# Two chains for the sums of squares, weight sums in small tiles, and other parts, in a two-layer hybrid decoder

## The chip, the cores and the metric

The kernel runs on one core of a Trainium2 chip. TensorE (PE, with its weight loads as PEld), VectorE (DVE), ScalarE (ACT) and GpSimd (POOL) each work through a queue of their own in order; transfers are issued from SyncE's queue (SP) and from GpSimd's. The metric is the device time of one execution in microseconds, the median of the runs.

## The reference

512 tokens of width 1024 pass through two layers, everything in float32:

```python
x = x + 0.5 * swiglu(rmsnorm(x, norm_ffn1[l]), w_ffn1_in[l], w_ffn1_out[l])
h = rmsnorm(x, norm_mix[l])
x = x + mixing_sublayer(h, w_in[l], ...)     # retention (4 heads) and forgetting attention (8 heads), gated
x = x + 0.5 * swiglu(rmsnorm(x, norm_ffn2[l]), w_ffn2_in[l], w_ffn2_out[l])
...
def rmsnorm(x, g): return x * rsqrt(mean(x * x) + EPS) * g
def swiglu(h, w_in, w_out):
    a, b = split(h @ w_in)                   # 2 x 2816 columns
    return (silu(a) * b) @ w_out
```

The output is rmsnorm of the last x.

## The kernel before

x is kept transposed, as eight tiles `x0` to `x7` of 128 channels by 512 tokens. Each float32 product is done as three matmuls of rounded halves: `split` makes the high half on ScalarE (a CAST, `wH`, `uH`, `xh`, `mh`) and the rest on VectorE (`wL`, `uL`, `ml`).

**FFN.** The 22 blocks of 128 hidden columns are taken in groups of four (some of two), and groups are put together into parts (`FF_PARTS`): a part's input products are followed by its output products (`po`), four times two blocks of x (`mi`). The input products of a group (`ffn_group`) are done as a 2 x 2 Strassen-like scheme: seven products of sums of weight quarters (`A12`, `A11`, `A22`, and the sums `S1`, `S3`) with seven forms of x (`b21`, `n11`, `m1` to `m4`, `b22`), into the banks Y, X and W. `prep_forms(n, l, k)` makes the forms of x tiles k and k+4, when these are done. `S1` and `S3` are made by a load of one quarter from SP and a transfer from GpSimd that adds another one (`summed`, L386); VectorE makes further sums with `more` (L425). A group's first weights, A12, are split into tiles of a ring: `wtile(w, ring[0])` takes every fourth pair of halves from the `y` tiles of the mixer and the forms, the others from the `wH` and `wL` tiles.

**Raw weights** lie in tiles that depend on `places`, and in two large `wst` tiles. With `aside`, in a group that follows the mixer and in the first of all, S1 lies in `wide` tiles.

**Statistics.** For the rmsnorm, `square` writes the square of each x tile (from three `r` tiles) on ScalarE and adds it to the first square, `sqa`, by a transfer from GpSimd. `rstd` sums `sqa` over its partitions with four matmuls `xs` (L315), then takes the root on GpSimd. In the mixer, R is the row of roots, sent to DRAM and read back for all partitions.

**Mixer** (`mix`): retention's values first (`rv_units`: 48 matmuls `pv` on the first half of the input blocks, then 48 on the second), then its heads, then the eight heads of forgetting attention, the gates and the outputs (`pyr`, `pyf`), and the product with `w_out` (`pw`), after which the forms of ffn2 are made.

The order on each engine is made from this code by a scheduler that may move instructions ahead of those that wait.

Of the kernel before, what the change touches and what calls it, by code (L numbers as in the profile page):

```python
# [6 lines left out]
F32 = mybir.dt.float32  # L7
FR = mybir.dt.float32r
AF = mybir.ActivationFunctionType
ALU = mybir.AluOpType  # L10
# [11 lines left out]
NFF = DFF // P  # L22
FF_PARTS = (((0, 4), (4, 4)), ((8, 4), (12, 4)), ((16, 2), (18, 4)))
FF_FIRST = (((2, 4),), ((6, 4), (10, 4)), ((14, 4), (18, 4)))
RH = 4
FH = 8
FD = 64
# [14 lines left out]
def trunk(  # L42
# [103 lines left out]

    xs = [st("x", f"x{m}") for m in range(KD)]
    xH, xL = [None] * KD, [None] * KD
    sqa = [None]


    def split(src, hi, lo, lo_eng=None):
# [25 lines left out]
        return w  # L178

    ALL = slice(None)  # L180

    def pair(nm, parts, nk=KD):

# [20 lines left out]
    def proj_tok(o, b, w, k0, nk, last_k, mvH, mvL):  # L204

        h, lo = w
        bs = slice(b * P, (b + 1) * P)
        for k in range(nk):
            kk = k0 + k
            PE.matmul(o, mvH[kk][:, bs], h[:, k], start=kk == 0, stop=False)  # L210
            PE.matmul(o, mvH[kk][:, bs], lo[:, k], start=False, stop=False)
            PE.matmul(o, mvL[kk][:, bs], h[:, k], start=False, stop=kk == last_k)  # L212


    def square(src, first):
        sq = st("r", "sq")
        S.activation(sq, src, AF.Square)
        if first:
            sqa[0] = sq
        else:  # L220
            G.dma_start(sqa[0], sq, accum_op=ALU.add)

    def prep(n, l, m):
        g = gain(n, l, m)
# [7 lines left out]
        square(src, m == 0)  # L232

# [15 lines left out]
    def prep_forms(n, l, k, first=False):  # L249

        if k == 0:
            tags[0] = iter(FIRST_TAGS if first else FORM_TAGS)
            forms.clear()
        x1, x2 = xs[k], xs[k + 4]
        H2 = T // 2
        b2 = st2(next(tags[0]), f"b2_{k}")
        scaled(b2[:, 0:T], b2[:, T:2 * T], x2, gain(n, l, k + 4))
        if k % 2 == 0:
            forms["n1", k // 2] = st2(next(tags[0]), f"n1_{k}")
        n1 = forms["n1", k // 2][:, (k % 2) * T:(k % 2 + 1) * T]  # L260
# [13 lines left out]
        V.scalar_tensor_tensor(  # L274
            out=m4, in0=x2[:, 0:H2], scalar=gain(n, l, k + 4), in1=m2,
            op0=ALU.mult, op1=ALU.subtract,
        )
        mh, ml = st2(next(tags[0]), f"mh{k}"), st2(next(tags[0]), f"ml{k}")
        split(mt, mh, ml)
        for q in range(2):  # L280
            def at(t, c):
                return t[:, c + q * P:c + (q + 1) * P]
            forms["b21", k, q] = at(b2, 0), at(b2, T)
            forms["b22", k, q] = at(b2, H2), at(b2, T + H2)
            forms["n11", k, q] = at(n1, 0), at(n1, H2)
            for i in range(4):
                forms[f"m{i + 1}", k, q] = at(mh, i * H2), at(ml, i * H2)
        if not first:
            square(x1, k == 0)
            square(x2, False)  # L290

    def to_dram(cols, n, nm):

# [61 lines left out]
    def ffn_group(w, f, n, todo, rtok, aside):  # L355
# [3 lines left out]
        nh = 4 // nk  # L359
        ca, cb = f * P, DFF + f * P  # L360

        def piece(r, c, s):
            return rows(w, r + s * nk * P, r + (s + 1) * nk * P, c, c + cw)

        def v3(t):
            return t.rearrange("p (k c) -> p k c", k=nk)

        def place(nm, tag=None):
            tag = tag or places[nm]
            nm = f"{nm}_{f}"  # L370
            if tag == "wst":
                t = wp.tile([P, 2048], F32, tag="wst", bufs=2, name=f"wst_{nm}")
                return [t[:, s * 1024:(s + 1) * 1024] for s in range(nh)]
            if tag == "wide":
                return [wide(f"{nm}_{s}")[:, 0:1024] for s in range(nh)]
            return [st2(tag, f"{nm}_{s}", F32) for s in range(nh)]

        def plain(ts, r, c):
            for s, t in enumerate(ts):
                load(v3(t), piece(r, c, s))  # L380
            return ts

        def summed(ts, r0, c0, r1, c1):
            for s, t in enumerate(ts):
                load(v3(t), piece(r0, c0, s))
                G.dma_start(v3(t), piece(r1, c1, s), accum_op=ALU.add)  # L386
            return ts

        K2 = 4 * P
        raw = {}  # L390
        raw["A12"] = plain(place("A12"), K2, ca)
        raw["A11"] = plain(place("A11"), 0, ca)
        raw["S1"] = summed(place("S1", "wide" if aside else None), 0, cb, K2, cb)
        raw["S3"] = summed(place("S3"), 0, ca, 0, cb)
        raw["A22"] = plain(place("A22"), K2, cb)
        next_places()

        def weights(nm):
            res = []
            for s in range(nh):  # L400
                h, lo = wtile("wH", ring[0]), wtile("wL", ring[0])
                ring[0] += 1
                split(raw[nm][s], h, lo)
                res.append((v3(h), v3(lo)))
            return res

        last_mm = [None]

        def mm(*args, **kw):
            last_mm[0] = PE.matmul(*args, skip_group_check=True, **kw).ins  # L410
# [10 lines left out]
                    mm(o, sl, h, start=False, stop=k == 3)  # L421

        def more(nm, by, out):
            for s in range(nh):
                V.tensor_tensor(out=raw[out][s], in0=raw[nm][s], in1=raw[by][s], op=ALU.add)  # L425
            raw[nm + by] = raw[out]

        def halves_of(t):
# [57 lines left out]
    def ffn_in(rtok, w, groups, aside, u):  # L486

        todo = []
        for i, (f, n) in enumerate(groups):
            ub = ffn_group(w, f, n, todo, rtok, aside and i == 0)  # L490
            todo = [
                lambda ub=ub, js=js: [turned(ub, j, u) for j in js]
                for js in (range(0, n // 2), range(n // 2, n))
            ]
        return todo

    def ffn_plain(w, mk):
# [5 lines left out]
        for jj in range(2):  # L503
            o = acc("pa")
            proj(o, cha[jj], xH, xL)
            t = st("t", "t1")
            V.tensor_tensor(out=t, in0=o, in1=R, op=ALU.mult)
            s = st("a", "sil")
            S.activation(s, t, AF.Silu)
            sil.append(s)  # L510
        chb = mk(w, DFF)
        for jj in range(2):
            o = acc("pb", True)
            proj(o, chb[jj], xH, xL)
# [18 lines left out]

    def ffn(l, which, w_i, w_o, done, paired, first=None):
        rtok = lazy(lambda: rstd(sqa[0], D, "x"))
        parts = FF_FIRST if first else FF_PARTS
        new_places(("xh",) * 4 if first else ("v", "v", "qk", "qk"))
        for pi, groups in enumerate(parts):
            last = pi == len(parts) - 1
            u = []  # L540
            if first and pi == 0:
                u, rt = ffn_plain(w_i[l], first)
                rtok = lambda: rt
            todo = ffn_in(rtok, w_i[l], groups, pi == 0 and (first or which == 2), u)
            if first and pi == 0:
                rest_of_constants()
            f1 = groups[-1][0] + groups[-1][1]
# [45 lines left out]
    def ffn_last(l, w_i, w_o):  # L593
# [68 lines left out]
        for pi, groups in enumerate(FF_PARTS):  # L662
            last = pi == len(FF_PARTS) - 1
            u = []
            todo = ffn_in(rtok, w_i[l], groups, pi == 0, u)
            f0, nf = groups[0][0], sum(n for _, n in groups)

            def product(o, b, unit, c0=0, c1=T):
# [42 lines left out]

    def mix(l):
        w = w_in[l]
        rtok = rstd(sqa[0], D, "x")
        R = bcast(flat(to_dram(rtok, TB, "r")), "r", "R")

        def vproj(c0, nm):

# [301 lines left out]
                    res.append(lambda i=i: weigh(h - 1, i))  # L1020
            return res

        for f in rv_units + rqk(0):
            f()
        interleave(retain(0), rqk(1) + rgate(0))
        forget()
# [60 lines left out]
        V.tensor_tensor(out=o, in0=ssx[:, 0:TB], in1=ssx[:, TB:2 * TB], op=ALU.add)  # L1087
        return o

    def first_pair(w, c0):  # L1090

        t = wp.tile([P, 2048], F32, tag="wst", bufs=2, name="wst_first")
        t = t.rearrange("p (k c) -> p k c", k=KD)
        for k in range(0, KD, 4):
            load(t[:, k:k + 4], rows(w, k * P, (k + 4) * P, c0, c0 + 2 * P))
        res = []
        for jj in range(2):
            res.append([
                wp.tile([P, 1024], FR, tag=tag, bufs=WB, name=f"{tag}_first")
                .rearrange("p (k c) -> p k c", k=KD) for tag in ("wH", "wL")  # L1100
            ])
        for jj in range(2):
            for k in range(0, KD, 4):
                split(
                    t[:, k:k + 4, jj * P:(jj + 1) * P],
                    *(x[:, k:k + 4] for x in res[jj]),
                )
        return res

    def inputs():  # L1110
        for hf in range(2):
# [12 lines left out]
                xH[m], xL[m] = hl("xh", f"xh{m}")  # L1124
                scaled(xH[m], xL[m], xs[m], gain(0, 0, m))
            for b in range(TB):
                sq = st("a", "sq")
                c = hf * TB + b
                S.activation(sq, xi[b], AF.Square, accum_out=ssx[:, c:c + 1])

# [67 lines left out]
```

## Time and profile before

| | |
|---|---|
| median of 3 runs | 2270.22 us (2266.68 to 2270.5) |
| profiled execution | 2271.86 us, of which span 2270.1 us |
| TensorE busy | 2189.3 us (96%), 10199 matmuls |
| VectorE, ScalarE, GpSimd busy | 1372.7, 998.1, 393.9 us |
| granted TensorE clock, mean | 0.982 of full speed |
| DMA, mean | 130 GB/s |

Busy time counts an engine's own work, not its waits nor the issue of transfers. Where TensorE is idle, the trace names what ended its wait. The granted clock is given as a share of full speed.

### The profile page before, as it was taken

How to read it: one execution, taken by the hardware profiler on the slowest of the kernel's cores; microseconds unless marked ns; L12 is line 12 of the kernel's file. 1: busy time of each engine (PE TensorE's matmuls, PEld its weight loads, DVE VectorE, ACT ScalarE, POOL GpSimd, SP SyncE). 2: the span in 40 equal slices, each digit the busy share in tenths (PEclk: the TensorE clock that was granted, in tenths of full speed). 3: DMA queues.
4: the chain of work that ended last, by engine and by line, in shares of the span. 5: the costliest groups of instructions: out<-in, count | busy, mean ns of one | idle time of the engine just before them, and what ended most of it. 6: DMA issues, size and time to landing. Idle time of an engine off the chain costs nothing.

```text
span 2270.1 us, 26380 instructions
## 1 busy us (share of the span) xinstructions
PE 2189.3 (96%) x10199; PEld 1817.8 (80%) x10199; DVE 1372.7 (60%) x1901; ACT 998.1 (44%) x1423; POOL 393.9 (17%) x323
## 2 busy tenths in 40 slices
PE   7999998999999989999989999989999998999998
PEld 5788887888878878888868888878888886888887
DVE  7566574456854675656666574646577546647564
ACT  6444353335542453444544353433454434535343
POOL 0010001454221210001010101015532221100001
PEclk9999999999999999999999999999999998999999
DMA  7576425324313685546665555153332228746441
GB/s 231 130 185 167 128 76 135 93 70 117 93 61 93 171 214 146 151 140 145 179 153 149 154 153 133 63 127 101 94 89 93 75 85 217 194 121 167 130 112 65
DMA packets 232085, 295.07 MB, mean 130 GB/s; under 512 B 10916, under 2 KB 138760, under 8 KB 231960
## 3 DMA queue, kind: packets, MB, share of 16 engines
q1 hardware_dynamic: 201992, 239.12, 33.6%
q0 software_dynamic: 29968, 54.27, 14.1%
q8 instruction: 80, 1.31, 0.2%
q14 instruction: 45, 0.37, 0.0%
HBM read 282.03 MB, written 2.15 MB: 125 GB/s over the span
## 4 chain that ended last, share of the span: by engine, by line
PE 44%; DMA 3%; DVE 1%; ACT 1%; issue 1%; POOL 0%; SPq 0%; POOLq 0%; ACTq 0%; DVEq 0%
PE X L410 9%; PE W L410 5%; PE po L192 2%; PE po L193 2%; PE po L191 2%; PE Y L410 2%; PE po L674 1%; PE po L676 1%; PE po L675 1%; PE pg L193 1%; PE pg L191 1%; PE pg L192 1%; DMA S<-in_w_ffn_in 1%; PE uT L480 1%; DMA wst_S<-in_w_ffn_in 1%; PE pv L212 1%
## 5 line engine op out<-in xcount | busy, mean ns | idle before, releaser
L153 ACT CAST wH<-A 128x1024 fp32r<-128x1024 f32 x138 | 145.1, 1054 | 172.5 <-PE po L192 54.3
L154 DVE TENSOR_TENSOR wL<-A,wH 128x1024 fp32r<-128x1024 f32 x138 | 168.2, 1223 | 84.4 <-ACT wH L153 83.4
L410 PE MATMUL X<-wL,mh 128*128 128x512 f32 (+1 forms) x552 | 211.5, 383 | 5.2 <-DVE wL L154 5.1
L410 PE MATMUL X<-wH,mh 128*128 128x512 f32 (+1 forms) x552 | 206.5, 386 | 8.9 <-ACT c L439 6.0
L410 PE MATMUL X<-wH,ml 128*128 128x512 f32 (+1 forms) x552 | 210.5, 382 | 0.0
L192 PE MATMUL po<-uL,wH_o 128*128 128x512 f32 x528 | 206.6, 392 | 0.0
L193 PE MATMUL po<-uH,wL_o 128*128 128x512 f32 x528 | 201.7, 391 | 0.0
L191 PE MATMUL po<-uH,wH_o 128*128 128x512 f32 x528 | 196.9, 391 | 0.0
L386 POOL DMA_DIRECT2D S<-in_w_ffn_in x59 | 72.0, 1222 | 575.4 <-DMA S<-in_w_ffn_in 298.1
L153 ACT CAST wH_o<-wst_o 128x1024 fp32r<-128x1024 f32 (+1 forms) x72 | 70.5, 981 | 163.4 <-PE po L192 140.3
L410 PEld LDWEIGHTS X<-wH,mh 128*128 128x128 f32 x552 | 105.9, 192 | 31.6 <-ACT c L439 8.2
L154 DVE TENSOR_TENSOR wL_o<-wst_o,wH_o 128x1024 fp32r<-128x1024 f32 (+1 forms) x72 | 81.5, 1133 | 81.8 <-ACT wH_o L153 81.7
L410 PEld LDWEIGHTS X<-wL,mh 128*128 128x128 f32 x552 | 106.0, 192 | 26.4 <-DVE wL L154 7.1
L410 PE MATMUL Y<-wH,b 128*128 128x512 f32 (+1 forms) x368 | 112.6, 380 | 14.7 <-ACT wH L153 14.7
L410 PEld LDWEIGHTS X<-wH,ml 128*128 128x128 f32 x552 | 106.1, 192 | 19.4
L153 ACT CAST wH<-wst_A 128x1024 fp32r<-128x1024 f32 x77 | 80.6, 1051 | 89.7 <-DVE wst_A L425 36.0
L154 DVE TENSOR_TENSOR wL<-wst_A,wH 128x1024 fp32r<-128x1024 f32 x77 | 93.8, 1222 | 36.9 <-ACT wH L153 35.6
L191 PEld LDWEIGHTS po<-uH,wH_o 128*128 128x128 f32 x528 | 99.1, 188 | 20.5
L192 PEld LDWEIGHTS po<-uL,wH_o 128*128 128x128 f32 x528 | 99.2, 188 | 20.1
L193 PEld LDWEIGHTS po<-uH,wL_o 128*128 128x128 f32 x528 | 99.0, 188 | 20.0
L410 PE MATMUL X<-wH,n 128*128 128x512 f32 (+1 forms) x368 | 114.8, 387 | 0.0
L410 PE MATMUL W<-wH,b 128*128 128x512 f32 (+1 forms) x368 | 114.4, 375 | 0.0
(311 smaller groups left out, 5549.4 us busy)
## 6 DMA issues: line engine op xcount, KB each, us to landing
A<-in_w_ffn_in SPq DMA_DIRECT2D x84, 512.0 KB
S<-in_w_ffn_in SPq DMA_DIRECT2D x59, 512.0 KB
S<-in_w_ffn_in POOLq DMA_DIRECT2D x59, 512.0 KB, 8.6
wst_o<-in_w_ffn_out SPq DMA_DIRECT2D x24, 1024.0 KB
wst_A<-in_w_ffn_in SPq DMA_DIRECT2D x45, 512.0 KB
wst_g<-in_w_in SPq DMA_DIRECT2D x16, 1024.0 KB
wst_S<-in_w_ffn_in SPq DMA_DIRECT2D x27, 512.0 KB
wst_S<-in_w_ffn_in POOLq DMA_DIRECT2D x27, 512.0 KB, 8.0
```

The costliest lines, as they stand in the source:

```text
L153: S.copy(hi, src)
L154: (lo_eng or V).tensor_tensor(out=lo, in0=src, in1=hi.bitcast(F32), op=ALU.subtract)
L191: PE.matmul(o, wh, mh, start=first, stop=False)
L192: PE.matmul(o, wh, ml, start=False, stop=False)
L193: PE.matmul(o, wl, mh, start=False, stop=last)
L212: PE.matmul(o, mvL[kk][:, bs], h[:, k], start=False, stop=kk == last_k)
L386: G.dma_start(v3(t), piece(r1, c1, s), accum_op=ALU.add)
L410: last_mm[0] = PE.matmul(*args, skip_group_check=True, **kw).ins
L480: PE.transpose(o[:, b * P:(b + 1) * P], ub[b][:, j * P:(j + 1) * P], ident)
L674: PE.matmul(o, uh, hh, start=k + i == 0, stop=False)
L675: PE.matmul(o, uh, ll, start=False, stop=False)
L676: PE.matmul(o, ul, hh, start=False, stop=k + i == nf - 1)
```

## The change

1. The sum of squares is made in two chains: the even tiles add into one square, the odd ones into another, squares 2 to 7 lie in `t` tiles, and VectorE adds both sums at the end.
2. In the mixer, the statistics are written behind the first 48 products, instead of ahead of them.
3. In the first group of all, of ffn2 of layer 0 and of the last FFN, S1 and S3 lie in four small `a` tiles each, 128x512, and `summed`, `weights` and `more` take them piece by piece. The first weights of the start use `a` tiles for their second pair.
4. The FFN that is followed by another FFN's forms (ffn2 of layer 0) takes the parts `FF_PAIRED`, of 6, 8 and 8 blocks instead of 8, 8 and 6.
5. The ring of weight tiles starts at 0 in each FFN part.

```diff
+FF_PAIRED = (((0, 4), (4, 2)), ((6, 4), (10, 4)), ((14, 4), (18, 4)))
...
-    def square(src, first):
-        sq = st("r", "sq")
+    def square(src, i):
+
+        sq = st("r" if i < 2 else "t", "sq")
         S.activation(sq, src, AF.Square)
-        if first:
-            sqa[0] = sq
+        if i < 2:
+            sqa[i] = sq
         else:
-            G.dma_start(sqa[0], sq, accum_op=ALU.add)
+            G.dma_start(sqa[i % 2], sq, accum_op=ALU.add)
+        if i == KD - 1:
+            V.tensor_tensor(out=sqa[0], in0=sqa[0], in1=sqa[1], op=ALU.add)
...
-            if tag == "wide":
-                return [wide(f"{nm}_{s}")[:, 0:1024] for s in range(nh)]
+            if tag == "a":
+                return [st("a", f"{nm}_{s}") for s in range(2 * nh)]
             return [st2(tag, f"{nm}_{s}", F32) for s in range(nh)]
+
+        def piece(ts, r, c, s):
+            n = 4 // len(ts)
+            return (
+                ts[s].rearrange("p (k c) -> p k c", k=n),
+                rows(w, r + s * n * P, r + (s + 1) * n * P, c, c + cw),
+            )
...
-        raw["S1"] = summed(place("S1", "wide" if aside else None), 0, cb, K2, cb)
-        raw["S3"] = summed(place("S3"), 0, ca, 0, cb)
+        raw["S1"] = summed(place("S1", aside), 0, cb, K2, cb)
+        raw["S3"] = summed(place("S3", aside), 0, ca, 0, cb)
...
-                split(raw[nm][s], h, lo)
+                ts = raw[nm]
+                n = len(ts) // nh
+                for i in range(n):
+                    c = slice(i * 1024 // n, (i + 1) * 1024 // n)
+                    split(ts[s * n + i], h[:, c], lo[:, c])
...
     def ffn_in(rtok, w, groups, aside, u):
 
         todo = []
+        ring[0] = 0
...
-        parts = FF_FIRST if first else FF_PARTS
+        parts = FF_FIRST if first else FF_PAIRED if paired else FF_PARTS
...
     def mix(l):
         w = w_in[l]
-        rtok = rstd(sqa[0], D, "x")
-        R = bcast(flat(to_dram(rtok, TB, "r")), "r", "R")
...
-        for f in rv_units + rqk(0):
+        rv_units[0]()
+        with tc.issue_after(last_mm[0]):
+            rtok = rstd(sqa[0], D, "x")
+            R = bcast(flat(to_dram(rtok, TB, "r")), "r", "R")
+        for f in rv_units[1:] + rqk(0):
             f()
...
-    def first_pair(w, c0):
-
-        t = wp.tile([P, 2048], F32, tag="wst", bufs=2, name="wst_first")
-        t = t.rearrange("p (k c) -> p k c", k=KD)
-        for k in range(0, KD, 4):
-            load(t[:, k:k + 4], rows(w, k * P, (k + 4) * P, c0, c0 + 2 * P))
+    def first_pair(w, c0, aside=False):
+
+        n = 2 if aside else 4
+        if aside:
+            ts = [st("a", "w0").rearrange("p (k c) -> p k c", k=n) for _ in range(4)]
```

TensorE's queue at the start of the first mixer, where the first half of retention's values (`pv`) ends; before:

```order
L210 MATMUL pv3_2788<-wH_rv001_2795,xh2_2606 128x512
L211 MATMUL pv3_2788<-wL_rv001_2796,xh2_2606 128x512
L212 MATMUL pv3_2788<-wH_rv001_2795,xh2_2606 128x512
L210 MATMUL pv3_2788<-wH_rv001_2795,xh3_2613 128x512
L315 MATMUL xs_2767<-ones_76,sq_2536 128x1 x4
L211 MATMUL pv3_2788<-wL_rv001_2796,xh3_2613 128x512
L212 MATMUL pv3_2788<-wH_rv001_2795,xh3_2613 128x512
```

And TensorE's queue there after the change:

```order
L214 MATMUL pv3_2806<-wH_rv001_2813,xh2_2640 128x512
L212 MATMUL pv3_2806<-wH_rv001_2813,xh3_2647 128x512
L213 MATMUL pv3_2806<-wL_rv001_2814,xh3_2647 128x512
L214 MATMUL pv3_2806<-wH_rv001_2813,xh3_2647 128x512
L322 MATMUL xs_2865<-ones_76,sq_2571 128x1 x4
L212 MATMUL pv0_2803<-wH_rv010_2884,xh4_2714 128x512
```

The matmuls on the sums of squares (`xs`) stood behind 46 of the 48 `pv` products of that half and now stand behind all 48.

GpSimd's queue just ahead of the first mixer, the transfers that add squares; before, with one sum, `sq_2536`:

```order
L221 DMA sq_2536<-sq_2609 128x512
L221 DMA sq_2536<-sq_2616 128x512
L221 DMA sq_2536<-sq_2683 128x512
L221 DMA sq_2536<-sq_2690 128x512
L221 DMA sq_2536<-sq_2757 128x512
L221 DMA sq_2536<-sq_2764 128x512
L324 TENSOR_TENSOR rsx_2773<-msx_2772,mhalf_78 128x4
```

And GpSimd's queue there after the change:

```order
L226 DMA sq_2571<-sq_2643 128x512
L226 DMA sq_2577<-sq_2650 128x512
L226 DMA sq_2571<-sq_2717 128x512
L226 DMA sq_2577<-sq_2724 128x512
L226 DMA sq_2571<-sq_2791 128x512
L226 DMA sq_2577<-sq_2798 128x512
L331 TENSOR_TENSOR rsx_2871<-msx_2870,mhalf_78 128x4
```

The transfers go by turns into `sq_2571` and `sq_2577`, and there is one transfer less.

ScalarE's queue at the end of the first mixer, where the last forms (`b1`, `b2_3`, `mh3`) and the first weights of ffn2 are made; before:

```order
L217 ACTIVATE sq_6101<-x3_84 128x512
L153 CAST wH_73_6169<-wst_A11_0_6110 128x1024
L244 ACTIVATE b2_3_6085<-x7_88,gcol_74 128x512
L217 ACTIVATE sq_6104<-x7_88 128x512
L153 CAST mh3_6097<-mt_6092 128x1024
L153 CAST wH_72_6165<-wst_A11_0_6110 128x1024
```

And ScalarE's queue there after the change:

```order
L222 ACTIVATE sq_6135<-x3_84 128x512
L154 CAST wH_3_6216<-wst_A11_0_6145 128x1024
L251 ACTIVATE b2_3_6119<-x7_88,gcol_74 128x512
L222 ACTIVATE sq_6138<-x7_88 128x512
L154 CAST mh3_6131<-mt_6126 128x1024
L154 CAST wH_0_6178<-wst_A12_0_6142 128x1024
```

The first half of A12, `wH_0`, with which TensorE's Y begins, now stands last, behind `mh3`; before, its place held a part of A11, and A12's halves (`wH_70`, `wH_71`) stood further ahead.

## Rows read from the trace of the kernel before

**Rows 1.** TensorE's waits by what ended them: total, times, longest

```profile
PE xs L315 <- DMA sq<-sq: 15.0, 2, 7.7
PE Y L410 <- ACT wH L153: 14.7, 2, 9.4
PE W L410 <- ACT wH L153: 10.4, 2, 6.9
```

**Rows 2.** Six stretches: length, busy time per engine, granted clock, DMA

```profile
30.00:74.00 44.00, 28.32 (x95) 21.44 (x94) 35.04 (x49) 24.05 (x32) 5.04 (x4) 0.77 0.73 204
388.00:406.00 18.00, 10.63 (x35) 8.53 (x34) 2.61 (x3) 1.33 (x2) 1.99 (x3) 0.72 0.39 88
788.00:808.00 20.00, 12.30 (x42) 8.76 (x41) 9.70 (x10) 5.38 (x8) 3.36 (x3) 0.83 1.07 270
1140.00:1180.00 40.00, 31.92 (x118) 23.46 (x117) 24.57 (x28) 20.29 (x27) 8.02 (x7) 0.87 0.71 166
1511.00:1529.00 18.00, 10.33 (x35) 8.20 (x34) 4.70 (x7) 3.30 (x5) 1.90 (x2) 0.72 0.48 121
1898.00:1932.00 34.00, 23.81 (x78) 18.03 (x78) 17.99 (x19) 10.88 (x13) 6.99 (x7) 0.80 0.92 244
```

**Rows 3.** TensorE's timeline in the first mixer: start, length, idle before

```profile
396.43 1.83 PE L315 MATMUL xs<-ones,sq 128*128 128x1 f32 x8 [7.37 <-DMA sq<-sq]
...
398.70 0.63 PE L212 MATMUL pv<-wH_rv,xh 128*128 128x512 f32 x1
...
404.22 0.40 PE L210 MATMUL pv<-wH_rv,xh 128*128 128x512 f32 x1
404.45 0.40 PE L211 MATMUL pv<-wL_rv,xh 128*128 128x512 f32 x1
```

**Rows 4.** The squares' tile, 340 to 400 us

```profile
DMA to landing us min/median/max: 3.3/5.2/7.1
```

**Rows 5.** ScalarE's timeline ahead of the first mixer

```profile
386.72 0.63 ACT L217 ACTIVATE sq<-x 128x512 f32<-128x512 f32 x1 [5.23 <-DMA sq<-sq]
```

**Rows 6.** GpSimd's timeline there

```profile
387.21 0.86 POOL L221 DMA_DIRECT2D sq<-sq  x1 [6.79 <-DMA sq<-sq]
391.06 0.87 POOL L221 DMA_DIRECT2D sq<-sq  x1 [2.98 <-issue]
```

**Rows 7.** TensorE's timeline at the start

```profile
46.53 1.22 PE L410 MATMUL Y<-wH,b 128*128 128x512 f32 x2 [9.45 <-ACT wH L153]
...
65.24 1.28 PE L410 MATMUL X<-wH,mh 128*128 128x512 f32 x2 [4.70 <-ACT c L439]
67.47 0.79 PE L410 MATMUL X<-wL,mh 128*128 128x512 f32 x1 [0.94 <-DVE wL L154]
```

**Rows 8.** VectorE's timeline at the start

```profile
32.27 0.68 DVE L154 TENSOR_TENSOR wL_first<-wst_first,wH_first 128x512 fp32r<-128x512 f32 x1
32.87 1.22 DVE L154 TENSOR_TENSOR wL<-wst_A,wH 128x1024 fp32r<-128x1024 f32 x1
...
39.53 0.48 DVE L270 SCALAR_TENSOR_TENSOR mt<-x,ncol,b 128x256 f32<-128x256 f32 x1
...
62.34 1.23 DVE L425 TENSOR_TENSOR wst_A<-S,wst_A 128x1024 f32<-128x1024 f32 x1 [5.71 <-DMA S<-in_w_ffn_in]
```

**Rows 9.** SP's timeline ahead of ffn2, layer 0

```profile
778.21 1.05 SPq L101 DMA_DIRECT2D S<-in_w_ffn_in  x2
```

**Rows 10.** TensorE's timeline at the last FFN

```profile
1904.15 1.22 PE L410 MATMUL Y<-wH,b 128*128 128x512 f32 x2 [5.25 <-ACT wH L153]
```

**Rows 11.** ScalarE's timeline at the last FFN

```profile
1902.11 1.04 ACT L153 CAST mh<-mt 128x1024 fp32r<-128x1024 f32 x1 [1.21 <-DVE mt L274]
1903.06 1.04 ACT L153 CAST wH<-wst_A 128x1024 fp32r<-128x1024 f32 x1
```

**Rows 12.** ScalarE's waits from 1120 to 1150 us

```profile
ACT sq L217 <- DMA sq<-sq: 7.7, 5, 2.6
```

**Rows 13.** TensorE's timeline, last head's end, layer 0

```profile
659.73 0.28 PE L193 MATMUL po<-pH,v 128*128 128x128 f32 x1
```

More of the change, by code (lines that the diff above doesn't have):

```diff
@@ L148, in trunk @@
     xH, xL = [None] * KD, [None] * KD
-    sqa = [None]
+    sqa = [None, None]
     def split(src, hi, lo, lo_eng=None):
@@ L180, in trunk @@
     ALL = slice(None)
+    last_mm = [None]
     def pair(nm, parts, nk=KD):
@@ L211, in proj_tok @@
             PE.matmul(o, mvH[kk][:, bs], lo[:, k], start=False, stop=False)
-            PE.matmul(o, mvL[kk][:, bs], h[:, k], start=False, stop=kk == last_k)
-    def square(src, first):
-        sq = st("r", "sq")
+            last_mm[0] = PE.matmul(
+                o, mvL[kk][:, bs], h[:, k], start=False, stop=kk == last_k
+            ).ins
+    def square(src, i):
+        sq = st("r" if i < 2 else "t", "sq")
         S.activation(sq, src, AF.Square)
-        if first:
-            sqa[0] = sq
-        else:
-            G.dma_start(sqa[0], sq, accum_op=ALU.add)
+        if i < 2:
+            sqa[i] = sq
+        else:
+            G.dma_start(sqa[i % 2], sq, accum_op=ALU.add)
+        if i == KD - 1:
+            V.tensor_tensor(out=sqa[0], in0=sqa[0], in1=sqa[1], op=ALU.add)
     def prep(n, l, m):
@@ L231, in prep @@
         )
-        square(src, m == 0)
+        square(src, m)
     forms = {}
@@ L288, in prep_forms @@
         if not first:
-            square(x1, k == 0)
-            square(x2, False)
+            square(x1, 2 * k)
+            square(x2, 2 * k + 1)
     def to_dram(cols, n, nm):
@@ L360, in ffn_group @@
         ca, cb = f * P, DFF + f * P
-        def piece(r, c, s):
-            return rows(w, r + s * nk * P, r + (s + 1) * nk * P, c, c + cw)
         def v3(t):
@@ L373, in place @@
                 return [t[:, s * 1024:(s + 1) * 1024] for s in range(nh)]
-            if tag == "wide":
-                return [wide(f"{nm}_{s}")[:, 0:1024] for s in range(nh)]
+            if tag == "a":
+                return [st("a", f"{nm}_{s}") for s in range(2 * nh)]
             return [st2(tag, f"{nm}_{s}", F32) for s in range(nh)]
+        def piece(ts, r, c, s):
[4 more added lines that the diff above has]
+            )
         def plain(ts, r, c):
             for s, t in enumerate(ts):
-                load(v3(t), piece(r, c, s))
+                load(*piece(ts, r, c, s))
             return ts
@@ L384, in summed @@
             for s, t in enumerate(ts):
-                load(v3(t), piece(r0, c0, s))
-                G.dma_start(v3(t), piece(r1, c1, s), accum_op=ALU.add)
+                load(*piece(ts, r0, c0, s))
+                G.dma_start(*piece(ts, r1, c1, s), accum_op=ALU.add)
             return ts
@@ L402, in weights @@
                 ring[0] += 1
-                split(raw[nm][s], h, lo)
+                ts = raw[nm]
[3 more added lines that the diff above has]
+                    split(ts[s * n + i], h[:, c], lo[:, c])
                 res.append((v3(h), v3(lo)))
             return res
-        last_mm = [None]
         def mm(*args, **kw):
@@ L423, in more, with bit @@
         def more(nm, by, out):
-            for s in range(nh):
-                V.tensor_tensor(out=raw[out][s], in0=raw[nm][s], in1=raw[by][s], op=ALU.add)
+            n = max(len(raw[nm]), len(raw[by]))
+            def bit(ts, s):
+                m = n // len(ts)
+                z = ts[0].shape[1] // m
+                return ts[s // m][:, s % m * z:(s % m + 1) * z]
+            for s in range(n):
+                V.tensor_tensor(
+                    out=bit(raw[out], s), in0=bit(raw[nm], s), in1=bit(raw[by], s), op=ALU.add
+                )
             raw[nm + by] = raw[out]
@@ L488, in ffn_in @@
         todo = []
+        ring[0] = 0
         for i, (f, n) in enumerate(groups):
-            ub = ffn_group(w, f, n, todo, rtok, aside and i == 0)
+            ub = ffn_group(w, f, n, todo, rtok, aside if i == 0 else None)
             todo = [
@@ L507, in ffn_plain @@
             V.tensor_tensor(out=t, in0=o, in1=R, op=ALU.mult)
-            s = st("a", "sil")
+            s = st("p", "sil")
             S.activation(s, t, AF.Silu)
             sil.append(s)
-        chb = mk(w, DFF)
+        chb = mk(w, DFF, True)
         for jj in range(2):
@@ L543, in ffn @@
                 rtok = lambda: rt
-            todo = ffn_in(rtok, w_i[l], groups, pi == 0 and (first or which == 2), u)
+            todo = ffn_in(
+                rtok, w_i[l], groups, "a" if pi == 0 and (first or which == 2) else None, u
+            )
             if first and pi == 0:
@@ L664, in ffn_last @@
             u = []
-            todo = ffn_in(rtok, w_i[l], groups, pi == 0, u)
+            todo = ffn_in(rtok, w_i[l], groups, None if pi else "a", u)
             f0, nf = groups[0][0], sum(n for _, n in groups)
@@ L1088, in sums @@
         return o
-    def first_pair(w, c0):
-        t = wp.tile([P, 2048], F32, tag="wst", bufs=2, name="wst_first")
-        t = t.rearrange("p (k c) -> p k c", k=KD)
-        for k in range(0, KD, 4):
-            load(t[:, k:k + 4], rows(w, k * P, (k + 4) * P, c0, c0 + 2 * P))
+    def first_pair(w, c0, aside=False):
+        n = 2 if aside else 4
+        if aside:
+            ts = [st("a", "w0").rearrange("p (k c) -> p k c", k=n) for _ in range(4)]
+        else:
+            t = wp.tile([P, 2048], F32, tag="wst", bufs=2, name="wst_first")
+            t = t.rearrange("p (k c) -> p k c", k=KD)
+            ts = [t[:, k:k + n] for k in range(0, KD, n)]
+        for i, t in enumerate(ts):
+            load(t, rows(w, i * n * P, (i + 1) * n * P, c0, c0 + 2 * P))
         res = []
@@ L1102, in first_pair @@
         for jj in range(2):
-            for k in range(0, KD, 4):
+            for i, t in enumerate(ts):
                 split(
-                    t[:, k:k + 4, jj * P:(jj + 1) * P],
-                    *(x[:, k:k + 4] for x in res[jj]),
+                    t[:, :, jj * P:(jj + 1) * P],
+                    *(x[:, i * n:(i + 1) * n] for x in res[jj]),
                 )
@@ L1126, in inputs @@
             for b in range(TB):
-                sq = st("a", "sq")
+                sq = st("r", "sq")
                 c = hf * TB + b
```

## The prediction

> **What bounds the kernel now.** I read the list of TensorE's waits first [rows 1], then busy time and granted clock around the longest of them [rows 2], then what each one ends on. TensorE is busy for 2189.3 of 2270.1 us (table above) and the change takes no matmul away, so only its idle time and its slow stretches can be won. The reader is to see in [rows 1] that the three largest entries are six waits in all: two before the mixers' sums of squares (15.0 us), two for the first weights of a group (14.7), two for the sums of weights (10.4). [rows 2] cuts out the six places where they lie, in order of time: the start (A), the first mixer (B), ffn2 of layer 0 (C), ffn1 of layer 1 (D), the second mixer (E), the last FFN (F). Window less busy time is 15.7, 7.4, 7.7, 8.1, 7.7 and 10.2 us: 56.8 idle.
>
> A long wait also costs afterwards. In B the granted clock is 0.72 over the window. From 398.70 to 404.22 thirteen 128x512 matmuls stand 0.43 us apart (1.2 GHz), and 0.23 from there on (2.4 GHz) [rows 3]: 13 x 0.2 = 2.6 us. I charge 2.6 for each wait of 3.5 us or more: two in A (9.45 and 4.70, [rows 7]), two in F (5.25, [rows 10], and the other 4.9), one elsewhere. So before: A 20.9, B 10.0, C 10.3, D 10.7, E 10.3, F 15.4, in all 77.6 us.
>
> **B and E, the sums of squares.** The order shows the matmuls on the sums only two places later than before: TensorE already did 46 of the 48 products first. Two matmuls are 0.45 us, no answer to a wait of 7.4. What moves its end is the two chains. Before, seven transfers add into one tile, each waits for the landing of the one before, and a landing takes 3.3 to 7.1 us [rows 4]. ScalarE has three tiles for squares, so it idles 5.23 us before the last square [rows 5], and the last two transfers are issued at 387.21 and 391.06 [rows 6]. After, squares 2 to 7 have five tiles of another kind, and the last two add into different sums. The last square can run where ScalarE now goes idle, at 386.72 - 5.23 = 381.49, and its transfer be issued at 382. With the longest landing of the row it is there at 389.1, and VectorE's new addition of the two sums (0.7, the 128x512 row in [rows 8]) ends at 389.8. TensorE arrives at 396.43 - 7.37 + 0.45 = 389.5. So 0 to 0.3 us of 7.37 is left, and no slow stretch. E has the same wait of the same cause, so the same sum. Bounds: nothing left (20.3 won), or half the waits left with their slow clock (10 won). I take 20.0, by the issue times. What follows TensorE's wait (the root, its row to DRAM and back) is issued no later than before and hidden by the 48 products of the second half, 10.9 us. Behind VectorE's addition stands the low half of the last weight, due 24 matmuls later.
>
> **F and C, the first group behind a mixer.** The weight sums are loaded from 778.21 on now [rows 9], and W waits 6.9 us for weights split from them [rows 1]. After, these loads stand right behind `neg7`, in tiles that are free with the last product of the last head, at 659.73 [rows 13]: 118 us earlier. Their eight additions (0.87 us of issue each, [rows 6], 7 in all) lie between the gate sums on GpSimd, and the eight loads stand ahead of a gate weight on SP. What hides both are the products of the next two outputs and two gates, whose weights stand ahead in the queue: 96 matmuls, 21.8 us. Without this cover they cost 7 us per mixer.
>
> But the ring also starts at 0, and tile 0 of the ring is a `y` tile, which the last forms take first. In ScalarE's order `wH_0` stands last, behind `mh3`. That is so in F already: `mh` at 1902.11, `wH` at 1903.06 [rows 11], and Y starts at 1904.15 after 5.25 us [rows 10]. This wait stays in F, and C gets it: 5.25, 0.3 for a cast behind it, and 2.6, or 8.1 in each. Gain: C 2.2, F 7.3.
>
> **D, the paired last part.** Squares held ScalarE for 7.7 us [rows 12]. This goes: 48 products, 10.9 us, lie between pairs of squares, and there are more tiles and two chains. But Y, now without a wait, will wait for `wH_0` behind `mh3`, and here two sums of weights stand on VectorE ahead of the last form. By the prices of [rows 8], less 0.08 us, by which one instruction overlaps the next, from the last product on: output 0.6, a weight's low half 1.14, four pieces of forms and a low half at 0.4, another low half 0.66, two weight sums at 1.14, with hand-overs 6.9 to the last form; then two casts on ScalarE of 1.0 [rows 11]: 9.0. With 0.3 and 2.6 it is 11.9 against 10.7, a loss of 1.2. Bounds: 5.25 as in F (a gain of 2.5), or 2 us more.
>
> The (4,2) group costs nothing: as many matmuls as before, and in its 168 half-width ones with 16 transposes (some 21 us) VectorE has 7 weights and 2 sums at 1.14, ten evictions at 0.4 and 4 low halves at 0.6: 16.7. Without that cover, 2.4.
>
> **A, the start.** The first weights and sums no longer wait for the second pair's large tile. Now VectorE idles 5.71 us for the sums [rows 8], and X stands 4.70 and 0.94 us [rows 7]. After, these waits go. But the order now puts on VectorE between the last `pb` product (46.53 - 9.45 = 37.1) and the last form that Y needs: five sums (four at 0.6, one at 1.14), a weight 1.14, four pieces of 0.6 and eleven of 0.4, 11.5 in all, in 0.3 after 37.1: 48.9. Then `mh0`, `mh1` and `wH_0` on ScalarE at 1.0 give Y at 51 or 52, against 46.53. So 14 idle and 2.6 slow, and some 0.3 because half a MB more stands ahead of the last input: 16.9 against 20.9, a gain of 4.0. Bounds: -3 (Y 7 us later still) to +8 (Y where it was).
>
> The Trainium skill, Perfetto Trace Analysis, DMA Optimizations, speaks against the small tiles: small transfers have an overhead of their own, larger ones use the memory better. [rows 4] shows that overhead as 3.3 us at least for 256 KB. By the rule the sums at the start could come late, the second rival; by the row they come in time.
>
> **The sum.** A 4.0, B and E 20.0, C 2.2, D -1.2, F 7.3: 32.3 us. The profiled execution took 2271.86 (1.8 outside its span, 1.6 above the median of 2270.22), so 2239.6: I say 2240. From no change a measurement tells about 0.2%, 4.5 us.
>
> **The rivals.**
> *The waits in B and E stay by half* (0.15): two transfers in flight land no sooner than one after the other, 7.1 us each, so that the last is there some 4 us late in both, with slow clocks: 10 of 20 us lost, 2250. For it: landings of up to 7.1. Against: the row's least is 3.3.
> *The start loses* (0.13): the small transfers of S run one after the other at 7.1 us, the first four from about 22 (estimate) to 50, where VectorE wants them by 43; Y comes 7 us later still, and A gives -3 for +4: 2247.
> *Y starts sooner* (0.06): in C, D and F the forms are done earlier than [rows 11] has them, 2.6 us each: 2232.
> *Slower* (0.05): VectorE's new addition in C, D and F waits for the last square's transfer, which in C and F GpSimd issues behind a transfer that waits for its own load. Weights for X stand behind this addition. It decides at 15 us after the last product, until when Y and X have work; each us beyond is lost. Landings of 7.1 lose nothing. At 28 us in three places 39 are lost: 2279.
> *It does not do what it says* (0.04): the waits of B, E and W stay, each behind another landing: 2270.
>
> **Chances.** My forecast, 2234 to 2246, has 0.57. Faster by over 0.2% are it and the first three rivals, 0.91; the same 0.04; slower 0.05. The range is 2231 to 2256: from the soonest Y to the half-kept waits with 6 us of new small ones. It leaves out about 0.15.
>
> **What would show it.** Right: no wait before the matmuls on the sums of squares in either mixer, and the clock at 1.00 there; no wait of W for sums; one wait before Y's first matmul of 5, 9 and 5 us in C, D and F, and of some 14 at the start. Wrong: over 2 us at the sums of squares; Y waiting 12 us or more in C or F; waits of X for weights behind VectorE's addition; new gaps in the (4,2) group or between the gates of a mixer.

## The result and the profile after

The changed kernel takes 2230.33 us (median of 4 runs, 2229.63 to 2233.17) against 2269.57 of the kernel before beside it: a ratio of 0.9832, 95% interval 0.9815 to 0.9849. The sign was forecast, and the mechanisms but for that at the start; the gain is 39.2 us where I had worked out 32.3, and the median lies 0.7 us below the low end of my range. The profiled execution took 2233.17 us (span 2231.4), 38.7 less than that of before.

The page's busy times, and TensorE's waits by what ended them (total, times, longest), answer to the table of before and to [rows 1]. Behind them stand the waits of X before, which [rows 1] doesn't show:

```profile
PE 2169.5 (97%) x10199; PEld 1807.5 (81%) x10199; DVE 1378.7 (62%) x1928; ACT 998.0 (45%) x1439; POOL 395.8 (18%) x330
```

```profile
PE Y L424 <- ACT wH L154: 39.5, 4, 19.9
PE xT L1155 <- DMA xi<-in_x: 5.5, 3, 4.3
PE po L193 <- DVE o L155: 4.8, 2, 2.4
...
PE W L424 <- ACT wH L154: 0.5, 2, 0.3
```

```profile
PE X L410 <- DVE wL L154: 7.6, 5, 3.0
PE X L410 <- ACT c L439: 6.0, 3, 4.7
...
PE X L410 <- ACT wH L153: 2.8, 2, 1.9
```

Three of the kinds of wait are gone or nearly so: `xs` for squares is not in the list, W for sums is down from 10.4 to 0.5, and X, with 16.4 us in ten waits before, is not in the list after. One has grown: Y for its first weight, from 14.7 us in two waits to 39.5 in four. Busy time fell by 19.8 us though the number of matmuls is the same: matmuls at the low clock take longer, and fewer of them run there.

The windows at A to F after, in order of time (length, busy time of PE, PEld, DVE, ACT, POOL, granted clock, DMA share, GB/s), answer to [rows 2]:

```profile
28.00:80.00 52.00, 32.07 (x134) 26.09 (x133) 37.55 (x59) 28.59 (x43) 6.16 (x7) 0.80 0.66 179
382.00:400.00 18.00, 18.00 (x85) 14.88 (x84) 6.19 (x8) 5.09 (x6) 1.05 (x1) 1.00 0.40 92
766.00:788.00 22.00, 16.75 (x62) 13.36 (x61) 15.83 (x21) 8.42 (x11) 3.12 (x3) 0.84 0.89 241
1117.00:1150.00 33.00, 23.92 (x93) 19.19 (x92) 21.84 (x26) 13.59 (x17) 1.71 (x2) 0.84 0.23 54
1478.00:1496.00 18.00, 18.00 (x86) 14.89 (x85) 5.74 (x9) 4.53 (x6) 2.74 (x3) 1.00 0.63 144
1863.00:1890.00 27.00, 21.49 (x84) 16.92 (x83) 19.46 (x27) 12.14 (x17) 4.25 (x4) 0.87 0.81 220
```

B and E are filled at a clock of 1.00. A, C, D and F are not.

Both programs have 10,199 matmuls, most of one size, and the order around each place is alike. So the start of the n-th matmul can be set against that of the n-th of the other trace, which counts waits and slow clock (the time at the lower of TensorE's two clocks) together:

| stretch, n-th matmul | before, start to end us | after | gained | forecast |
|---|---|---|---|---|
| start to 300 (A) | 0 to 97.32 | 0 to 96.31 | 1.0 | 4.0 |
| 300 to 1600 | to 383.23 | to 382.49 | -0.3 | 0 |
| 1600 to 1800 (B) | to 438.74 | to 426.77 | 11.2 | 10.0 |
| 1800 to 3400 | to 779.10 | to 768.17 | -1.0 | 0 |
| 3400 to 3600 (C) | to 834.68 | to 820.70 | 3.1 | 2.2 |
| 3600 to 5000 | to 1125.26 | to 1111.95 | -0.7 | 0 |
| 5000 to 5200 (D) | to 1184.16 | to 1168.65 | 2.2 | -1.2 |
| 5200 to 6600 | to 1476.19 | to 1459.04 | 1.6 | 0 |
| 6600 to 6800 (E) | to 1532.02 | to 1503.44 | 11.4 | 10.0 |
| 6800 to 8400 | to 1872.22 | to 1842.11 | 1.5 | 0 |
| 8400 to 8800 (F) | to 1977.03 | to 1938.64 | 8.3 | 7.3 |
| 8800 to the end | to 2270.1 | to 2231.4 | 0.3 | 0 |

Together 38.7 (with the digits that the table rounds off). In one place the count itself shifts time: eight of the 200 matmuls of C are half as wide after as before, since the group of two blocks comes earlier. That puts 0.9 us too much into C's gain, and as much too little into that of the stretch behind: C gained 2.2, and that stretch 0.2. Of the 6.4 us between forecast and profile B and E make 2.7, D 3.4, F 1.0, the stretches for which I had nothing 2.4, and the start takes 3.0 back. That the last two nearly cancel is luck.

### The profile page after: what moved, and what is told of

Its sections match the earlier page's. It is cut to its first block, busy times and chain, and to the rows that moved or that the text cites. A ratio compares the mean times of both kernels' runs of the same rounds, so it can differ in the third digit from the quotient of the medians.

```text
span 2231.4 us, 26468 instructions
## 1 busy us (share of the span) xinstructions
PE 2169.5 (97%) x10199; PEld 1807.5 (81%) x10199; DVE 1378.7 (62%) x1928; ACT 998.0 (45%) x1439; POOL 395.8 (18%) x330
## 4 chain that ended last, share of the span: by engine, by line
PE 95%; DVE 2%; ACT 1%; DMA 1%; issue 1%; SPq 0%; POOLq 0%; ACTq 0%
PE X L424 21%; PE W L424 10%; PE po L194 6%; PE po L195 6%; PE po L193 6%; PE Y L424 5%; PE pg L195 3%; PE pg L193 3%; PE pg L194 3%; PE uT L503 2%; PE po L700 1%; PE po L702 1%; PE po L701 1%; PE prq L193 1%; PE pv L212 1%; PE pv L213 1%
## 5 line engine op out<-in xcount | busy, mean ns | idle before, releaser
L424 PE MATMUL X<-wL,mh 128*128 128x512 f32 (+1 forms) x552 | 206.9, 375 | 0.0
L424 PE MATMUL X<-wH,mh 128*128 128x512 f32 (+1 forms) x552 | 201.0, 376 | 0.0
L398 POOL DMA_DIRECT2D S<-in_w_ffn_in x71 | 80.4, 1198 | 607.7 <-DMA S<-in_w_ffn_in 362.8
L424 PE MATMUL Y<-wH,b 128*128 128x512 f32 (+1 forms) x368 | 114.3, 383 | 39.5 <-ACT wH L154 39.5
L424 PE MATMUL X<-wH,n 128*128 128x512 f32 (+1 forms) x368 | 119.4, 395 | 0.0
L194 PEld LDWEIGHTS po<-uL,wH_o 128*128 128x128 f32 x528 | 99.2, 188 | 19.8
```

Source lines behind the costliest of these rows:

```text
L194: PE.matmul(o, wh, ml, start=False, stop=False)
L398: G.dma_start(*piece(ts, r1, c1, s), accum_op=ALU.add)
```

## The experiments

Each kernel was timed beside the kernel before. The time of that kernel was 2269 to 2271.4 us in these sets, so I give medians and ratios. My theory: the mixers' waits were the length of a chain of landings (not the place of the statistics); in C, D and F what is left is Y's first weight behind the last forms; at the start something came late that I had not counted. The rivals stand with each run.

**Two chains with their tiles, on the kernel before** (edits 2 to 5 left out).

```diff
-        sq = st("r", "sq")
+        sq = st("r" if i < 2 else "t", "sq")
...
+            G.dma_start(sqa[i % 2], sq, accum_op=ALU.add)
```

> The kernel before with the squares in two chains and t tiles alone, statistics written where they were. If the chain of landings is what held TensorE in both mixers, the waits of 7.37 and 7.67 us and their slow stretches go here already: 20 to 23 us faster than before. If the place of the statistics behind the products is needed too, at least half of the waits stays: 10 us or less. If the squares matter in the FFN's paired part too (ScalarE's 7.7 us there), up to 3 us more.

2249.87 us, ratio 0.9910 (0.9895 to 0.9924): 19.3 faster. Neither `xs` wait is in its trace; counted by the n-th matmul, B gives 11.2 and E 11.4, the same as in the changed kernel. It stays a little below 20: this profile lost 4.0 us at the start, where nothing was edited, and 2.0 in C. So the place of the statistics isn't needed.

**The tiles alone**: squares 1 to 7 in `t` tiles, one sum.

```diff
-        sq = st("r", "sq")
+        sq = st("r" if i < 1 else "t", "sq")
```

> The kernel before with squares 1 to 7 in t tiles, but still one sum into which seven transfers add one after the other. If it is the number of chains that counts, the last two transfers still stand behind one another, 5.2 us each: about half of the gain, 8 to 12 us. If it was the lack of tiles that held ScalarE, the waits go as with two chains: 18 us or more.

2267.38 us, ratio 0.9990 (0.9981 to 0.9999), and no half of the gain: the two waits became 17.4 us from 15.0. TensorE's waits, and GpSimd's timeline (start, length, idle before it and what ended it):

```profile
PE xs L316 <- DMA sq<-sq: 17.4, 2, 8.7
```

```profile
382.87 0.86 POOL L222 DMA_DIRECT2D sq<-sq  x1 [6.60 <-DMA sq<-sq]
386.80 0.86 POOL L222 DMA_DIRECT2D sq<-sq  x1 [3.08 <-DMA sq<-sq]
393.78 0.87 POOL L222 DMA_DIRECT2D sq<-sq  x1 [6.12 <-issue]
```

ScalarE, no longer held, ended its last square at 380.2, but each transfer still waits for the landing before it, and the seventh landed at 397.10. Squares made sooner only queue up ahead of GpSimd. That holds for the mixers: in D the one profile of this kernel is 7.8 us shorter than before. The profiled execution took 2263.5 us, the second fastest of ten; their median, 1.8 us faster than before, doesn't bear out so much.

**The statistics behind the products, alone.**

```diff
-        rtok = rstd(sqa[0], D, "x")
...
+        rv_units[0]()
+        with tc.issue_after(last_mm[0]):
+            rtok = rstd(sqa[0], D, "x")
...
```

> The kernel before with the statistics of the mixers written behind the first 48 products, and nothing else. By my working two matmuls more stand ahead of the sums, 0.45 us per mixer: 0 to 1 us faster, within 0.2%. If the place in the queue is what the change lives on, 10 us faster or more.

2269.93 us, ratio 1.000 (0.999 to 1.001). Its two waits, of 7.33 and 7.82 us, are about those of before. Counted by the n-th matmul, B gains 0.5 and E 0.6, near the 0.45 that was worked out; the medians can't tell that from nothing.

**Two chains without the tiles**: all squares in the three `r` tiles.

```diff
-        sq = st("r" if i < 2 else "t", "sq")
+        sq = st("r", "sq")
```

> The kernel before with two chains, but all squares in the three r tiles as before: the two sums hold two of them, so one is left for the six squares that are added. Tiles alone changed nothing in the mixers (8.6 and 8.7 us stay). If the chains alone are the cure, 2248 to 2252 us as with chains and tiles together (2249.9). If both are needed, each square now waits for the transfer of the one before out of the single tile, landing after landing, and the waits of 7 us or more stay in both mixers: 2262 us or more.

2255.26 us, ratio 0.9932 (0.9915 to 0.9948). Both expectations missed. One tile is left, the transfers do go one after the other, yet only 2.04 and 2.43 us of wait remain. TensorE's row, and GpSimd's last two:

```profile
394.07 1.02 PE L318 MATMUL xs<-ones,sq 128*128 128x1 f32 x8 [2.04 <-DVE sq L224]
...
382.07 0.86 POOL L222 DMA_DIRECT2D sq<-sq  x1 [3.63 <-ACT sq L218]
389.71 0.86 POOL L222 DMA_DIRECT2D sq<-sq  x1 [6.78 <-ACT sq L218]
```

Two sums need six transfers where one needs seven, and the sixth landed at 393.14, 3.2 us sooner than the seventh of before. Counted by the n-th matmul, B gains 9.0 and E 7.2 here, of 11.2 and 11.4 with the tiles: the shorter chain is worth 16 of 22.7 us in the mixers, and the overlap that the tiles allow the other 6.5. The tiles matter in C and F too. There ScalarE now waits 12.0 and 11.2 us for the one tile, and this profile loses 5.2 us in C and 2.5 in F; D is 5.0 shorter.

**Small tiles for the sums in C and F, alone** (start, ring and squares as before).

```diff
+            if tag == "a":
+                return [st("a", f"{nm}_{s}") for s in range(2 * nh)]
...
```

> The kernel before with S1 and S3 in small a tiles in the first group of ffn2 of layer 0 and of the last FFN alone; start, ring and squares as before. If W and X there waited for these sums only, C's 9 us and the 4.9 us in F with its slow stretch go: 15 to 17 us faster. If another wait comes in their place (a first weight behind the last forms, as Y's 5.25 us in F), half of it stays: 7 to 10 us.

2254.21 us, ratio 0.9934 (0.9919 to 0.9948), 15 us faster. In C, TensorE's 6.9 us for W are gone and one wait of 2.50 for a low half is left; in F only Y's 5.25 remain. The early loads do what they should, and C was then cheaper than in the changed kernel: there something else takes some of it back.

**No start of the ring at 0.**

```diff
-        ring[0] = 0
```

> The changed kernel without the ring's start at 0. If the start at 0 puts Y's first weight behind the last forms in C, as I reckoned, C's wait of 5.25 us with its slow stretch (2.4) goes, F keeps its own, and in D the second half of A12 is late instead of the first: 2220 to 2226 us. If the weight is not what Y waits for in C, but the last forms themselves, the same time as the changed kernel, 2230 within 3 us.

2221.16 us, ratio 0.9780 (0.9765 to 0.9794): 9.2 us faster than the changed kernel by the medians, 11.8 by the ratios. TensorE's waits for Y's first weight are two, at the start and in F:

```profile
PE Y L424 <- ACT wH L154: 22.7, 2, 17.4
```

C has none any more, nor has D, of which I had expected only a shorter one; F keeps 5.26. By the n-th matmul C is 6.0 us and D 10.4 shorter than in the changed kernel, and the stretch between them, with the group of two blocks, 3.4 longer. This line of the change is a loss.

**The ring started at 1**, so that A12 is never in a `y` tile.

```diff
-        ring[0] = 0
+        ring[0] = 1
```

> The changed kernel with the ring started at 1 in each part, so that both halves of A12 lie in weight tiles and are split ahead of the last forms, and the second half of A11 takes the y tile. If the weight alone is what Y waits for in C, D and F, 5.25, 9.08 and 5.25 us and their slow stretches (2.4, 2.6, 2.0) go, 26 us, less what X then waits for A11: 2204 to 2214 us. If Y then waits for the last forms, or X as long for A11, half or less is won: 2217 us or more.

2215.04 us, ratio 0.9752 (0.9736 to 0.9769): 15.3 faster than the changed kernel by the medians, 18.2 by the ratios. The median lies 1 us outside the near edge of the first expectation and short of the second. In C, D and F no wait for Y's first weight is left. ScalarE there, in C:

```profile
766.79 1.05 ACT L154 CAST wH<-wst_A 128x1024 fp32r<-128x1024 f32 x1 [2.84 <-issue]
...
770.14 1.06 ACT L154 CAST mh<-mt 128x1024 fp32r<-128x1024 f32 x1 [1.16 <-DVE mt L281]
771.10 2.04 ACT L154 CAST wH<-wst_A 128x1024 fp32r<-128x1024 f32 x2
```

The weights behind `mh3` are now A11's, which X wants later. What comes in place: X stands 1.54 us in C and 2.34 in F for low halves, the first output product of the paired FFN stands 2.58 for its raw weights, and at the start Y begins at 37.3, stands 2.11 for a low half and then 10.07 for a form, until 56.15. So the group of two blocks, free in the changed kernel, is not free here.

**The old parts in ffn2 of layer 0.**

```diff
-        parts = FF_FIRST if first else FF_PAIRED if paired else FF_PARTS
+        parts = FF_FIRST if first else FF_PARTS
```

> The changed kernel with the old parts in ffn2 of layer 0, the last one of 6 blocks. In the two-chain kernel with the old parts TensorE waited 7.9 us in D in all, and with single sums and more tiles 4.3; the changed kernel waits 9.1. If the larger last part does not count, as the wait for Y's weight is the end there: 2230 within 3 us. If it is what keeps the squares out of ScalarE's way: 4 us slower or more.

2235.81 us, ratio 0.9846 (0.9832 to 0.9861), 3.2 slower than the changed kernel by the ratios and 5.5 by the medians. TensorE's waits in D:

```profile
PE Y L424 <- ACT wH L154: 14.7, 1, 14.7
```

That is 5.6 us more than the 9.08 of the changed kernel: the larger last part does count, and my first expectation was wrong.

**The ring at 1 and the old parts.**

> The ring started at 1 with the old parts in ffn2 of layer 0 (2215 us with the new ones). If the larger last part only shortens the wait of Y for its first weight in D (9.1 for 14.7 us), it is worth nothing where that weight is early, and the waits around the group of two blocks (2.6 and 0.9 us) go too: 2211 to 2214. If the squares and forms themselves press with the smaller last part, D waits again 4 us or more: 2217 or more.

2216.95 us, ratio 0.9768 (0.9754 to 0.9783), against 0.9752: 2 to 4 us slower, which is near the noise, and nearer to the second expectation. The waits around the group of two blocks went, but D waits 0.80 and 3.42 with 2.4 of slow clock behind them, as the second expectation had it. By the n-th matmul D is 5.4 us longer than with the ring at 1 alone, C and the stretch with the group of two blocks together 2.6 shorter. So even with the early weight the larger part seems worth a little.

**The start as before**, but for the tiles of the squares of the input.

```diff
-        chb = mk(w, DFF, True)
+        chb = mk(w, DFF)
...
+                rtok, w_i[l], groups, ("wide" if first else "a" if which == 2 else None) if pi == 0 else None, u
```

> The changed kernel with the start as before: S1 in wide tiles and the first weights' second pair in a large tile. My prediction has the new start 4 us better: 2234. By the trace of the changed kernel the new start only changes one wait for another (19.9 us for Y in place of 9.5, 4.7 and 0.9, and one slow stretch of 1.4 in place of two of 2.4): 2230 to 2232. If the sums loaded early cost more than they save, 2228 or less.

2233.21 us, ratio 0.9835 (0.9820 to 0.9849) against 0.9832: 0.7 us by the ratios, 2.9 by the medians. Y waits 9.77, X 5.69 and 1.52, for one wait of 19.93. Counted to the 300th matmul this start takes 98.4 us, the new one 96.3. One profile says little here: the runs that keep the start of before reach it at 96.9 to 101.3, and those with the changed one (the changed kernel, no start of the ring at 0, the old parts) at 94.5 to 96.5. So the new start is worth some 2 us, and less than my 4.

**The start's row of roots by TensorE**, on the changed kernel.

```diff
-        R = bcast(flat(to_dram(rtok, TB, "r")), "r", "R")
...
+            V.tensor_scalar(
+                out=dg, in0=ident, scalar1=rtok[:, b:b + 1], scalar2=None, op0=ALU.mult
+            )
+            PE.matmul(ro[:, b * P:(b + 1) * P], on, dg, start=True, stop=True)
+        R = st("r", "R")
+        V.tensor_copy(R, ro)
```

> The changed kernel, with the row of roots at the start made by four matmuls on TensorE (a matrix of ones by a diagonal of roots) instead of being sent to DRAM and read back. In the changed kernel VectorE stood 5.91 us until 37.39 for that row, with 16.3 us of work behind it before the last form that Y needs. If the late row is why Y starts at 56 and not at 51 or 52, VectorE begins at about 31, Y starts 5 to 7 us sooner: 2223 to 2226 us. If it is VectorE's work alone, which would only be shifted, or ScalarE's order: 2229 or more.

2226.25 us, ratio 0.9816 (0.9799 to 0.9832), 4.1 faster by the medians. VectorE's first products with the row, and TensorE's Y:

```profile
30.57 1.28 DVE L541 TENSOR_TENSOR t<-pa,R 128x512 f32<-128x512 f32 x2
...
50.21 1.22 PE L424 MATMUL Y<-wH,b 128*128 128x512 f32 x2 [13.91 <-ACT wH L154]
```

Y starts 5.8 us sooner, and its wait is the 14 us that the prediction had.

**The same row, and the ring at 1.**

> The same row by TensorE with the ring started at 1 (2215 us with the row through DRAM). There Y already started at 40 us and stood 10.1 us later for a form. If the form was late for the same reason, 4 to 6 us are won: 2209 to 2211. If that wait has another cause: 2214 or more.

2210.21 us, ratio 0.9741 (0.9727 to 0.9756): the fastest, 20.1 us under the changed kernel. The form for which Y stands came at 51.99 instead of 56.15, so it was late for the same reason.

## Why the prediction was right, and where its sizes were off

**B and E: right, and more than I took.** In the changed kernel the last additions overlap. GpSimd's transfers and VectorE's addition of both sums, then TensorE, and the landings of the squares' tile (of before, [rows 4] and [rows 6]):

```profile
377.56 0.86 POOL L226 DMA_DIRECT2D sq<-sq  x1 [7.28 <-ACT sq L222]
380.30 0.86 POOL L226 DMA_DIRECT2D sq<-sq  x1 [1.89 <-ACT sq L222]
...
384.68 0.69 DVE L228 TENSOR_TENSOR sq<-sq 128x512 f32<-128x512 f32 x1 [3.96 <-DMA sq<-sq]
...
388.61 0.95 PE L322 MATMUL xs<-ones,sq 128*128 128x1 f32 x8
```

```profile
DMA to landing us min/median/max: 3.3/4.1/5.8
```

GpSimd is now released by squares, not by landings. I had the last transfer issued at 382 and the sum done at 389.8, a hair late; it was issued at 380.30 and the sum was done at 385.4, with 3.2 us to spare. The place behind the products, which I took as worth 0.45 us, adds nothing to this: with the chains alone B and E are as short. The rival that two transfers in flight land no sooner than one after the other falls with the last two: issued 2.74 us apart, they landed 1.28 us apart. What I missed is 1.2 us per mixer: after a wait the matmuls on the sums themselves run at the low clock, 1.83 us in [rows 3] against 0.95 now, and two more products behind them are slow.

**C and F: the mechanism to the digit.** Both have Y's wait of 5.25 us for `wH_0` behind `mh3`, as reckoned from [rows 10] and [rows 11]. ScalarE's rows, in C, then in D, and TensorE's Y in C and in D:

```profile
775.16 1.04 ACT L154 CAST mh<-mt 128x1024 fp32r<-128x1024 f32 x1 [1.16 <-DVE mt L281]
776.11 1.04 ACT L154 CAST wH<-wst_A 128x1024 fp32r<-128x1024 f32 x1
...
1130.03 1.04 ACT L154 CAST mh<-mt 128x1024 fp32r<-128x1024 f32 x1 [3.47 <-DVE mt L281]
1130.99 1.04 ACT L154 CAST wH<-wst_A 128x1024 fp32r<-128x1024 f32 x1
...
777.21 1.22 PE L424 MATMUL Y<-wH,b 128*128 128x512 f32 x2 [5.25 <-ACT wH L154]
...
1132.08 1.22 PE L424 MATMUL Y<-wH,b 128*128 128x512 f32 x2 [9.08 <-ACT wH L154]
```

C gained 2.2 (3.1 in the table, less the 0.9 of the narrower matmuls), as forecast. F gained 8.3, 1.0 above mine, by the clock: the matmuls behind the waits of before lost 5.8 us to the low clock, where I had charged 5.2, and those behind the one wait of after 2.4 instead of 2.6. (The "other 4.9" us of before, which I took for one wait, are two of 1.93 and 3.00.) That the start of the ring at 0 brings this wait to C and to D is shown by the kernels with no such start and with 1.

**D: the wait right, the price of before wrong.** Y waits 9.08 us; I had worked out 9.0. The step that failed is the 10.7 us that I charged before the change: 200 matmuls from the 5000th on took 58.9 us there. At full clock 192 of them stand 0.227 us apart, and the eight of one column 0.11, which makes 44.5; so D cost 14.4 before and 12.2 after, where I had 10.7 and 11.9. I had charged 2.6 for one long wait, while the granted clock over the 40 us of D in [rows 2] was 0.87, which is 5.2 us: instead of one long wait six of 0.4 to 3.5 us lie there. So -1.2 became +2.2. That the (4,2) group costs nothing came out: TensorE stands 0.27 us in its stretch, against 0.24 before.

**A: the wrong step is "from the last product on".** I let VectorE's 11.5 us of work begin at 37.1, with its products with the row R done by then, as before. SP's timeline before, then after, VectorE's wait for that row, and TensorE's Y after:

```profile
24.06 0.28 SPq L101 DMA_DIRECT2D r_d<-rowsT  x1
25.26 0.34 SPq L101 DMA_DIRECT2D R<-r_d  x1
```

```profile
21.80 0.98 SPq L102 DMA_DIRECT2D wst_A<-in_w_ffn_in  x2
26.11 0.27 SPq L102 DMA_DIRECT2D r_d<-rowsT  x1
32.87 0.34 SPq L102 DMA_DIRECT2D R<-r_d  x1
...
37.39 1.29 DVE L531 TENSOR_TENSOR t<-pa,R 128x512 f32<-128x512 f32 x2 [5.91 <-DMA R<-r_d]
...
56.03 1.22 PE L424 MATMUL Y<-wH,b 128*128 128x512 f32 x2 [19.93 <-ACT wH L154]
```

Before, the row of roots went out at 24.06 and its reading back was issued at 25.26; now 6.76 us lie between the two, behind a megabyte of weights and four transfers of sums that start just ahead. VectorE stood until 37.39, with 16.4 us of work up to the last form, at 53.79, and Y began at 56.03 instead of 51 or 52. Of the 4.0 us 1.0 came in this profile. The run with the row by TensorE shows that the late row is the cause: Y begins at 50.2. In the run with the old start, where the weights are issued at 16.18 and the sums only at 32.74, the row goes out at 24.45 and its reading back is issued at 25.68. So the sums in small tiles did come in time, as the row of before had it, and cost the start elsewhere, by standing ahead of a small transfer.

The Trainium skill's rule on larger transfers (Perfetto Trace Analysis, DMA Optimizations), weighed in the prediction, decided nothing: no wait for a small sum is left. Nor did it bear on these transfers as I put it: that section of the Trainium skill speaks of an overhead of transfers below 2 KB, and the 3.3 us of [rows 4], which I called the overhead of 256 KB, are the whole time from issue to landing. Nearer is the Trainium skill, DMA: Bandwidth & Descriptors, Latency and other measured facts, which has the fixed part of a transfer grow where memory is loaded. The trace agrees in direction, 1.20 us against 6.76 for the same row, but no run here tells that part from queueing behind the weights.

**What I had nothing for.** Between the 5200th and 6600th matmul 1.6 us came from a wait of 1.71 before a low half; it is gone in the run with the statistics alone too, and in those with one other edit alone, so it hangs on the scheduler's order rather than on an edit. In the mixers' heads TensorE has the same wait of 2.39 us in both kernels. The granted clock around it was 0.83 before and 0.66 after in the first mixer, and 1.00 there in the run with the old parts; in the second mixer it was 0.83 before and 1.00 after. That answers to the 1.0 us lost and the 1.5 gained in the two long stretches that hold the mixers' heads. I know no edit that this follows from; it stays open.

The rival on the other side, X's weights behind VectorE's addition, did not come up: the addition waited 4.3 us for the last landing in C, 0.8 in D and 5.2 in F, and no wait of X is left behind it.

Of the signs named beforehand all came but one: at the start Y waited 19.93 us, not some 14.

## What to carry to other kernels

Where transfers accumulate into one tile, as the sums of squares do here, count the landings in series: more sources ready sooner bought nothing in the mixers (2267.4 of 2269.1 us in all), a chain made shorter by splitting the sum bought 14.8, and 19.3 together with the sources. When a load is moved ahead, look for the small transfer that it now overtakes: a row of roots here held VectorE for 6 us. And where a pool hands out tiles by turns, check which tensor lands in the tile that comes free last: the start of one counter was worth 15 us.

## What was not expected of the hardware

A row of 2 KB written to DRAM landed in 1.20 us or less where no weights were issued just ahead of it (24.06 to 25.26), and in up to 6.76 with weights and sums in flight. Two accumulating transfers into different tiles in flight together landed no later here than one alone: 3.3 to 5.8 us, against 3.3 to 7.1 one by one [rows 4]. After the unchanged wait of 2.39 us in the first mixer the granted clock was 0.66 in one profile and 1.00 in another over like windows of 10 us, which is 2.5 us between two profiles of what is the same code there; differences of that size in one profile tell nothing.
